# Gates and their output products as [token, column], and a 512-wide hi/lo product in the feed-forward inputs of a four-layer network on one core

## The chip, the cores and the metric

One NeuronCore of a Trainium2 chip runs the whole program. The metric is the device time of one execution in microseconds (us).

## The reference, cut to what matters

Two blocks of two layers each work on 256 tokens of 1024 columns, in float32. Every layer ends in the same two stages: gated attention branches that are mixed and projected back into the residual stream, and a feed-forward network.

```
# block 1 (layers 0, 1)
proj = rms_norm(x) @ w_in                       # 7984 columns for the attentions, then m_a, m_b (1024 each)
y_ret = (silu(g_r) * o_r) @ w_o_ret             # 2048 -> 1024
y_nsa = o_n @ w_o_nsa                           # 1024 -> 1024
x = x + (sigmoid(m_a)*y_ret + sigmoid(m_b)*y_nsa) @ w_out
a, b = split(rms_norm(x) @ w_ffn_in)            # 2 x 2816 columns
x = x + (silu(a) * b) @ w_ffn_out
# block 2 (layers 0, 1)
gates = sigmoid(gl)                             # three gates of 1024 columns
merged = sum over a, b, c of gate * (y @ w_br)  # each y: 512 -> 1024
x = x + merged @ w_out
x = x + square(relu(rmsnorm(x) @ w_up)) @ w_down        # 4096 columns
x = x + sigmoid(rmsnorm(x) @ w_ple_gate) * (p @ w_ple_proj)
```

## The kernel before, in words

**Three products for one.** Every float32 operand is split into `hi`, its value rounded to float32r, and `lo`, the rest. A product is then hi·hi + hi·lo + lo·hi, three float32r products added up in a PSUM bank. A weight piece of 512 KB is loaded by SP's DMA queue (`load`, L365), rounded into `whi` by ScalarE (ACT) and subtracted into `wlo` by VectorE (DVE) (`split_weight`, L377; the operations themselves stand at L169 and L183). `execute` (L391) writes out the program item by item; it splits pieces up to `LOOK` = 2 items ahead of their use. There are 5 raw and 6 split buffers.

**Two layouts.** `proj_T` (L442) keeps the weight stationary and streams the activations: per 128 rows and 128 columns of weight three products of 256 tokens each, and two column tiles share one bank of [128, 2, 256]. Its output is [column, token]. A unit of 256 columns on 1024 rows takes 8 x 2 x 3 = 48 products. `proj_N` (L479) keeps the activations stationary and streams 512 weight columns: the output is [token, column], one bank for each of the two token tiles t; 512 columns on 1024 rows take 8 x 2 x 3 = 48 products. `Down` (L526) has the form of `proj_N` with four banks [t][column half] that live through the whole feed-forward stage; `bulk` adds pieces as the hidden chunks come, `ends` does the last eight row tiles, first for column half 0, then for half 1. In the profile "b<-u,whi" is a product with stationary `whi` and streamed `u` (`proj_T`), "b<-whi,u" one with stationary `u` and streamed `whi` (`proj_N`, `Down`). PSUM has eight banks (`bank`).

**Block 1's gates** (`block1_layer`, L743; the stage begins after the heads). `ev_ma`, `ev_mb` put tanh(m/2) aside, `ev_yr` and `ev_yn` multiply (1 + tanh) with the branch's bank; the second adds the first, halves the sum and splits it into `mixT`, an `Act` of [column, token] that `w_out` then takes as its stationary operand. All four projections are `proj_T`; w_o_ret has 16 row tiles, the others 8. **Block 2's gates** (`block2_layer`, L1268: `ev_gates`, `ev_br`, `gates`, `branch`) do the same with three gates (8 row tiles) and three branches (4 row tiles).

**Feed-forward inputs.** Block 1: columns 0 to 255 of a and b go together through `proj_N`, which covers the transposes of the norm; the other ten chunks of 256 columns are `proj_T` units, a (evicted by Silu on ACT) and then b (multiplied from the bank on DVE, then split). Block 2: columns 0 to 511 by `proj_N`, then fourteen `proj_T` units (Relu on ACT, square on DVE, split).

**Norms and turns.** `Norm` (L594) scales x to [token, column]; `turn` transposes 128 x 128 blocks on TensorE (PE, L250) and splits them from PSUM into the hi and lo tiles of the next stream (hT, hF, hP), which are `u` tiles: the pool has 17 of 4 KB a partition. `first_turn` stands ahead of the last weight piece of the product before it; it also sets `order_after`, behind which later weight splits are issued.

**Order.** The instructions of each engine run in the order in which the program issues them. `Beside` (L291) holds generators for the small work (attention heads, transposes of results). `pump` advances them after every item by the planner's own costs; `until` and `finish` advance them until something is done. `begin` (L678) starts the kernel: x's first token tile on SP's queue, the norm's row and x's second token tile on ACT's queue, a constant, three warm-up products and two products that spread the norm's row over the partitions.

Of the kernel before, what the change touches and what calls it, by code (L numbers as in the profile page):

```python
# [18 lines left out]
D = 1024  # L19
# [62 lines left out]
NB_RAW, NB_HI, NB_U, NB_Z, NB_W, NB_S = 5, 6, 17, 6, 8, 24  # L82
# [20 lines left out]
def tile_kernel(ctx: ExitStack, tc: tile.TileContext, A: dict, out: bass.AP):  # L103
# [11 lines left out]
    def u(shape, dt=F32):  # L115
        return up.tile(shape, dt, name="u", tag="u", bufs=NB_U)

# [321 lines left out]

    S = {}  # L440

# [37 lines left out]
    def proj_N(w2d, c0, c, x, nkt, evac, runs=1, stride=0, tmajor=False, between=None, turn=None):  # L479
# [9 lines left out]
        def fn(pc, j, k0, nk, tt_):  # L489
            if tmajor and j == len(ks) - 1 and tt_ == (0,) and between is not None:  # L490
                between()
            for t in tt_:
# [33 lines left out]
    class Down:  # L526
# [26 lines left out]
        def ends(self, f, norm, turn=None):  # L553
# [4 lines left out]
            for j in pairs:  # L558
                def fn(pc, j=j):
                    for kk in range(2):  # L560
# [81 lines left out]

    def new_norm(row, key):

        def f():
            S["norm"] = Norm(row, None if key is None else Act(8))
            if key is not None:
                S["next", key] = S["norm"].dst
        do(f)
# [27 lines left out]

    def begin():  # L678
# [10 lines left out]
        consts(cp, 0)  # L689
# [4 lines left out]
        S["norm"] = Norm(None, Act(8), g=g)  # L694
# [48 lines left out]
    def block1_layer(i):  # L743
# [372 lines left out]
        def part(o, c):  # L1116
            if c % 2 == 0:
                o[c // 2] = u([128, 4, 256])
            return o[c // 2][:, 2 * (c % 2):2 * (c % 2) + 2, :]

        def half_of(o, c):
            return o[c // 2][:, 2 * (c % 2):2 * (c % 2) + 2, :]

        def ev_ma(c):
            def f(ci, acc):
                ma[c] = w2([128, 2, 256])
                act(ma[c], acc, AF.Tanh, scale=0.5)
            return f

        def ev_yr(c):  # L1130
            def f(ci, acc):
                stt(out=part(M, c), in0=ma.pop(c), scalar=1.0, in1=acc, op0=OP.add, op1=OP.mult)
            return f

        def ev_mb(ci, acc):
            act(part(G, ci), acc, AF.Tanh, scale=0.5)

        def ev_yn(c, acc):
            s = w2([128, 2, 256])
            stt(out=s, in0=half_of(G, c), scalar=1.0, in1=acc, op0=OP.add, op1=OP.mult)  # L1140
            tt(out=s, in0=s, in1=half_of(M, c), op=OP.add)
            cs = slice(2 * (c % 2), 2 * (c % 2) + 2)
            m = S["mixT"]
            split(s, m.hi[c // 2][:, cs, :], m.lo[c // 2][:, cs, :], 0.5)
# [17 lines left out]
        dn.ends("mixT", norm, lambda: first_turn("hF"))  # L1162
# [40 lines left out]
        def ev_a(ci, acc):  # L1203
            R["s"] = w2([128, 2, 256])
            act(R["s"], acc, AF.Silu)

        def ev_b(c):
            def f(ci, acc):
                s = R["s"]
                tt(out=s, in0=s, in1=acc, op=OP.mult)  # L1210
# [57 lines left out]
    def block2_layer(i):  # L1268
# [353 lines left out]
        def part(o, c):  # L1622
            if c % 2 == 0:
                o[c // 2] = u([128, 4, 256])
            return o[c // 2][:, 2 * (c % 2):2 * (c % 2) + 2, :]

        def half_of(o, c):
            return o[c // 2][:, 2 * (c % 2):2 * (c % 2) + 2, :]

        def ev_gates(b, raw):  # L1630
            def f(c, acc):
                if raw:
                    copy_a(part(G[b], c), acc)
                else:
                    act(part(G[b], c), acc, AF.Tanh, scale=0.5)
            return f

        def tanh_gates():
            for j in range(2):
                act(G["b"][j], G["b"][j], AF.Tanh, scale=0.5)  # L1640

        def ev_br(b):
            def f(c, acc):
                m = part(M, c) if b == "b" else w2([128, 2, 256])
                stt(out=m, in0=half_of(G[b], c), scalar=1.0, in1=acc, op0=OP.add, op1=OP.mult)
# [208 lines left out]
```

## Time and profile before

| | us |
|---|---|
| runs of the kernel before | 2163.63 median of 3 (2163.18 to 2164.15) |
| the profiled execution's own time | 2162.97 |
| its span in the profile | 2161.0 |
| PE busy | 2135.8 |
| DVE busy | 1488.0 |
| ACT busy | 1235.0 |

The granted clock of the span is 1.00 of 2.4 GHz. A product's duration in the profile (284 ns for one of 256 columns) holds the time through the array; products overlap, so what one costs is the distance from its start to the next one's. In the timeline, neighbouring instructions of one form are merged ("x2"), and the start is that of the first.

### The profile page before, as it was taken

To read this page: it belongs to the slowest core of one execution; us is meant where nothing else is said; L and a number is where in the kernel's file an instruction comes from. 1 tells how busy PE (TensorE), PEld (TensorE's weight loads), DVE (VectorE), ACT (ScalarE), POOL (GpSimd) and SP (SyncE) were. 2 spreads that over 40 slices of the span, in tenths; PEclk is the share of its full clock that TensorE was granted. 3 is DMA by queue.
4 is the path that set the end of the run, shared out by engine and by line. 5 is a ranking of instruction groups with operands and counts; after the bars stand their busy time and mean duration, and the time that the engine had idled before them with its cause. 6 is when DMAs were issued, how large, how long until landed. Compare 5 with 4: busy or idle time off the path is not lost.

```text
span 2161.0 us, 37493 instructions
## 1 busy us (share of the span) xinstructions
PE 2135.8 (99%) x14688; PEld 1952.0 (90%) x14688; DVE 1488.0 (69%) x2774; ACT 1235.0 (57%) x2044; POOL 97.8 (5%) x115
## 2 busy tenths in 40 slices
PE   9999999999999999999999999999999999999998
PEld 7898899899988889998997999998997999998997
DVE  6687865655577787666556897876557887876555
ACT  5476754544456666545445777755445777655443
POOL 1000000000000000000000010100000010100000
PEclk9999999999999999999999999999999999999999
DMA  9655555566585554555555645556655545455653
GB/s 284 204 157 145 150 166 168 185 187 188 175 261 156 150 156 136 167 192 176 185 186 167 185 126 161 159 173 197 186 186 172 171 136 176 152 185 179 191 186 108
DMA packets 298271, 376.49 MB, mean 174 GB/s; under 512 B 16364, under 2 KB 238588, under 8 KB 298094
## 3 DMA queue, kind: packets, MB, share of 16 engines
q1 hardware_dynamic: 296140, 369.07, 55.3%
q0 software_dynamic: 1664, 4.50, 1.2%
q8 instruction: 115, 1.88, 0.4%
q10 hardware_dynamic: 290, 0.53, 0.1%
q14 instruction: 62, 0.51, 0.1%
HBM read 372.93 MB, written 1.11 MB: 173 GB/s over the span
## 4 chain that ended last, share of the span: by engine, by line
PE 83%; DVE 10%; ACT 3%; issue 2%; POOL 1%; DMA 0%; POOLq 0%; SPq 0%; DVEq 0%; ACTq 0%
PE b L216 80%; DVE wlo L183 3%; PE b L250 3%; DVE u L183 2%; DVE w L183 1%; POOL s L239 1%; ACT z L169 1%; ACT u L169 1%; ACT whi L169 1%; DVE z L194 1%; DVE w L194 0%; DVE s L208 0%; DVE z L183 0%; ACT L169 0%; DVE z L1408 0%
## 5 line engine op out<-in xcount | busy, mean ns | idle before, releaser
L183 DVE TENSOR_TENSOR wlo<-raw,whi 128x1024 fp32r<-128x1024 f32 (+1 forms) x670 | 815.1, 1221 | 428.2 <-ACT whi L169 421.6
L169 ACT ACTIVATE whi<-raw 128x1024 fp32r<-128x1024 f32 (+1 forms) x670 | 704.9, 1056 | 655.2 <-PE b L216 460.6
L216 PE MATMUL b<-u,whi 128*128 128x256 f32 x5760 | 1049.3, 284 | 0.0
L216 PEld LDWEIGHTS b<-u,whi 128*128 128x128 f32 x5760 | 900.4, 192 | 9.5 <-issue 4.9
L216 PE MATMUL b<-u,wlo 128*128 128x256 f32 x2880 | 814.7, 283 | 0.0
L216 PE MATMUL b<-whi,u 128*128 128x512 f32 (+2 forms) x2752 | 809.1, 371 | 0.2
L216 PEld LDWEIGHTS b<-whi,u 128*128 128x128 f32 x2752 | 500.8, 189 | 88.6 <-issue 4.9
L216 PEld LDWEIGHTS b<-u,wlo 128*128 128x128 f32 x2880 | 552.0, 192 | 0.0
L216 PE MATMUL b<-wlo,u 128*128 128x512 f32 (+2 forms) x1376 | 508.4, 369 | 0.0
L216 PEld LDWEIGHTS b<-wlo,u 128*128 128x128 f32 x1376 | 259.9, 189 | 39.0 <-DVE wlo L183 0.9
L169 ACT ACTIVATE u<-b 64x512 fp32r<-64x512 f32 (+3 forms) x234 | 134.0, 579 | 86.7 <-PE b L250 44.4
L169 ACT ACTIVATE z<-z,s 128x256 f32<-128x256 f32 (+2 forms) x304 | 123.6, 425 | 25.5 <-DVE s L203 22.6
L239 POOL TENSOR_TENSOR s<-s,mhalf 128x1 f32<-128x1 f32 (+3 forms) x60 | 70.5, 1174 | 1491.8 <-DVE s L194 1060.2
L183 DVE TENSOR_TENSOR u<-b,u 128x512 fp32r<-128x512 f32 (+2 forms) x150 | 98.3, 665 | 12.0 <-ACT u L169 9.3
L169 ACT ACTIVATE w<-b 128x512 f32<-128x512 f32 (+3 forms) x150 | 81.1, 546 | 44.4 <-PE b L216 43.9
L250 PE MATMUL b<-const,w 128*128 128x128 f32 (+1 forms) x416 | 64.2, 279 | 11.3 <-DVE w L194 10.3
L250 PEld LDWEIGHTS b<-const,w 128*128 128x128 f32 (+1 forms) x416 | 47.7, 141 | 24.2 <-issue 13.7
L169 ACT ACTIVATE u<-w 128x512 fp32r<-128x512 f32 x80 | 49.5, 620 | 10.1 <-DVE w L183 9.9
L183 DVE TENSOR_TENSOR w<-w 128x512 f32<-128x512 f32 (+3 forms) x94 | 51.9, 566 | 3.3 <-ACT w L169 3.2
L169 ACT ACTIVATE w<-x 128x512 f32<-128x512 f32 x44 | 27.4, 623 | 32.6 <-DVE x L183 30.6
L216 PE MATMUL b<-u 128*128 128x256 f32 (+1 forms) x288 | 40.8, 287 | 3.4 <-DVE u L183 3.4
L183 DVE TENSOR_TENSOR u<-w,u 128x512 fp32r<-128x512 f32 x64 | 43.8, 685 | 0.0
(147 smaller groups left out, 1198.4 us busy)
## 6 DMA issues: line engine op xcount, KB each, us to landing
raw<-w_in SPq DMA_DIRECT2D x268, 512.0 KB, 3.8
raw<-w_ffn_in SPq DMA_DIRECT2D x80, 512.0 KB, 3.5
raw<-w_up SPq DMA_DIRECT2D x64, 512.0 KB, 3.7
raw<-w_down SPq DMA_DIRECT2D x64, 512.0 KB, 3.5
raw<-w_ffn_out SPq DMA_DIRECT2D x44, 512.0 KB, 3.6
raw<-w_o_ret SPq DMA_DIRECT2D x32, 512.0 KB, 3.5
raw<-w_out SPq DMA_DIRECT2D x32, 512.0 KB, 3.6
raw<-w_o_nsa SPq DMA_DIRECT2D x16, 512.0 KB, 3.4
```

Source lines behind the costliest of these rows:

```text
L169: nc.scalar.activation(o, i, func, bias=bias, scale=scale, accum_out=accum_out)
L183: nc.vector.tensor_tensor(out=out, in0=in0, in1=in1, op=op)
L194: nc.vector.scalar_tensor_tensor(out=out, in0=in0, scalar=scalar, in1=in1, op0=op0, op1=op1)
L216: nc.tensor.matmul(o, lhsT, rhs, start=start, stop=stop, skip_group_check=True)
L239: nc.gpsimd.tensor_tensor(o, i, mhalf[:, :n], op=OP.pow)
L250: nc.tensor.transpose(o, i, C("ident")[:i.shape[0], :i.shape[0]])
```

## The change: what it does

- `proj_T2` with `Stream` and `both_halves`: in the feed-forward inputs of both blocks, `whi` meets hi and lo of the stream in one 512-wide product, and `wlo` meets hi in a 256-wide one into the first half of the bank. There is a bank for each of the two column tiles, so two for a unit. The eviction copies the second half (ACT) and adds it to the first (DVE), for each bank. Block 2's Relu and square become one DVE operation.
- `Stream` lays hi and lo of the normed stream side by side in two tiles of a pool of their own (`xt`, two buffers of 8 KB a partition); the `u` pool shrinks from 17 to 13 buffers.
- Gates and branch products of both blocks become `proj_N` with 512 columns. `Mix` transposes the gated sums (four 128 x 128 transposes for each token tile and column half) and splits them into `mixT`; `need` makes `w_out`'s first pass wait for its half.
- `begin`: x's second token tile goes to SP's queue behind the first two weight pieces; the first norm's scaling is put ahead of the first weight split on DVE (`order_after`), and the second token tile's norm behind the first turn's last ACT instruction.

```diff
-NB_RAW, NB_HI, NB_U, NB_Z, NB_W, NB_S = 5, 6, 17, 6, 8, 24
+NB_RAW, NB_HI, NB_U, NB_X, NB_Z, NB_W, NB_S = 5, 6, 13, 2, 6, 8, 24
...
+    class Stream:
+        def __init__(self):
+            self.b = [xt([128, 2, 4, 256]) for _ in range(2)]
+            self.hi, self.lo = ([z[:, j] for z in self.b] for j in range(2))
...
+        def HL(self, k):
+            return self.b[k // 4][:, :, k % 4, :]
...
+    def proj_T2(w2d, c0, x, evac):
+        box = {}
+        for k0 in range(0, 8, 4):
+            def fn(pc, k0=k0):
+                if k0 == 0:
+                    box["b"] = [bank([128, 2, 256]) for _ in range(2)]
+                hi, lo = pc
+                for k in range(4):
+                    kk = k0 + k
+                    for ct in range(2):
+                        cs = slice(128 * ct, 128 * ct + 128)
+                        o = box["b"][ct]
+                        mm(o, hi[:, k, cs], S[x].HL(kk), kk == 0, False)
+                        mm(o[:, 0, :], lo[:, k, cs], S[x].H(kk), False, kk == 7)
+                if k0:
+                    evac(box["b"])
+            items.append(Item(fn, spec(w2d, 128 * k0, 4, c0, 256)))
+
+    def both_halves(banks):
+        s, h = w2([128, 2, 256]), w2([128, 2, 256])
+        for ct, b in enumerate(banks):
+            copy_a(h[:, ct, :], b[:, 1, :])
+            tt(out=s[:, ct, :], in0=b[:, 0, :], in1=h[:, ct, :], op=OP.add)
+        return s
...
+    class Mix:
+        def __init__(self):
+            S["mixT"], self.done = Act(8), set()
+        def turn(self, t, c, s):
+            def g():
+                yield
+                b = bank([128, 4, 128])
+                for q in range(4):
+                    transpose(b[:, q, :], s[:, 128 * q:128 * q + 128])
+                ts_ = slice(128 * t, 128 * t + 128)
+                split(b, S["mixT"].hi[c][:, :, ts_], S["mixT"].lo[c][:, :, ts_], 0.5)
+                self.done.add((t, c))
+                yield
+            bg.add(g(), True)
+        def need(self, k):
+            bg.until(lambda: all((t, k // 4) in self.done for t in range(2)))
...
     def begin():
-        for q, t in ((nc.sync, 0), (nc.scalar, 1)):
-            if t:
-                row = u([1, D])
-                q.dma_start(row, A["norm_mix_g"][0:1, :])
-            for c in range(2):
-                q.dma_start(x[:, t, 512 * c:512 * c + 512], xin[:, t, 512 * c:512 * c + 512])
+        row = u([1, D])
+        nc.scalar.dma_start(row, A["norm_mix_g"][0:1, :])
+        load_x(0)
+        consts(cp, 0)
+        for it in [z for z in items if z.spec is not None and not z.spec[-1]][:2]:
+            with tc.issue_after(last_of(mybir.EngineType.SP)):
+                it.pc = load(it.spec)
+        with tc.issue_after(last_of(mybir.EngineType.SP)):
+            load_x(1)
...
-        for c in range(4):
-            proj_T(w, 7984 + 256 * c, 256, "hT", 8, ev_ma(c))
-            if c:
-                proj_T(A["w_o_ret"][i], 256 * (c - 1), 256, "ret", 16, ev_yr(c - 1), pre=need_ret if c == 1 else None)
-        proj_T(w, 9008, 256, "hT", 8, ev_mb)
-        proj_T(A["w_o_ret"][i], 768, 256, "ret", 16, ev_yr(3))
-        for c in range(1, 4):
-            proj_T(w, 9008 + 256 * c, 256, "hT", 8, lambda ci, acc, c=c: ev_mb(c, acc))
+        for c in range(2):
+            proj_N(w, 7984 + 512 * c, 512, "hT", 8, ev_ma(c))
+            proj_N(A["w_o_ret"][i], 512 * c, 512, "ret", 16, ev_yr(c), pre=None if c else need_ret)
+        for c in range(2):
+            proj_N(w, 9008 + 512 * c, 512, "hT", 8, ev_mb(c))
         do(bg.finish)
-        do(lambda: S.update(mixT=Act(8)))
-        proj_T(A["w_o_nsa"][i], 0, 1024, "onT", 8, ev_yn)
+        do(lambda: S.update(mix=Mix()))
+        for c in range(2):
+            proj_N(A["w_o_nsa"][i], 512 * c, 512, "onT", 8, ev_yn(c))
...
-        dn.ends("mixT", norm, lambda: first_turn("hF"))
+        dn.ends("mixT", norm, lambda: first_turn("hF"), lambda j: S["mix"].need(j))
...
-                proj_T(wi, 256 * c, 256, "hF", 8, ev_a)
-                proj_T(wi, FFN + 256 * c, 256, "hF", 8, ev_b(c))
+                proj_T2(wi, 256 * c, "hF", ev_a)
+                proj_T2(wi, FFN + 256 * c, "hF", ev_b(c))
...
-                r = w2([128, 2, 256])
-                act(r, acc, AF.Relu)
-                tt(out=r, in0=r, in1=r, op=OP.mult)
+                r = both_halves(banks)
+                stt(out=r, in0=r, scalar=0.0, in1=r, op0=OP.max, op1=OP.mult)
...
+    def first_norm():
+        norm().both(0)
+        order_after[:] = [last_of(mybir.EngineType.DVE), last_of(mybir.EngineType.Activation)]
+
+    def second_norm():
+        with tc.issue_after(last_of(mybir.EngineType.Activation)):
+            norm().both(1)
```

## Rows read from the trace of the kernel before

**Rows 1.** The page: busy time of the engines, and the chain that ended last by engine.

```profile
PE 2135.8 (99%) x14688; PEld 1952.0 (90%) x14688; DVE 1488.0 (69%) x2774; ACT 1235.0 (57%) x2044; POOL 97.8 (5%) x115
...
PE 83%; DVE 10%; ACT 3%; issue 2%; POOL 1%; DMA 0%; POOLq 0%; SPq 0%; DVEq 0%; ACTq 0%
```

**Rows 2.** Waits of PE: waiting, releaser, us in total, times, longest.

```profile
PE b L250 <- DVE w L194: 10.3, 12, 3.4
```

**Rows 3.** Groups by form: line, engine, out<-in, stationary, streamed, count | busy us, mean ns.

```profile
L216 PE MATMUL b<-u,whi 128*128 128x256 f32 x5760 | 1049.3, 284 | 0.0
...
L216 PE MATMUL b<-u,wlo 128*128 128x256 f32 x2880 | 814.7, 283 | 0.0
...
L216 PE MATMUL b<-whi,u 128*128 128x512 f32 x2176 | 698.7, 393 | 0.2
...
L216 PE MATMUL b<-wlo,u 128*128 128x512 f32 x1088 | 426.1, 392 | 0.0
```

**Rows 4.** Timeline, PE, block 1's second layer, in a `proj_T` stretch.

```profile
900.00 0.40 PE L216 MATMUL b<-u,whi 128*128 128x256 f32 x2
...
904.68 0.40 PE L216 MATMUL b<-u,whi 128*128 128x256 f32 x2
```

**Rows 5.** Timeline, PE, in a `Down` stretch of the feed-forward stage.

```profile
429.71 0.62 PE L216 MATMUL b<-whi,u 128*128 128x512 f32 x2
...
432.43 0.62 PE L216 MATMUL b<-whi,u 128*128 128x512 f32 x2
```

**Rows 6.** Timeline, PE, a `proj_N` stretch in block 1's attention stage.

```profile
61.73 0.40 PE L216 MATMUL b<-whi,u 128*128 128x512 f32 x1
...
64.25 0.39 PE L216 MATMUL b<-whi,u 128*128 128x512 f32 x1
```

**Rows 7.** Timeline, PE, block 2: products whose streamed operand lies in two parts.

```profile
1234.98 1.11 PE L216 MATMUL b<-u,later 128*128 128x512 f32 x6
1235.93 0.40 PE L216 MATMUL b<-u,whi 128*128 128x256 f32 x2
```

**Rows 8.** Windows of the feed-forward stages: length, then busy us (instructions) by engine.

```profile
420.00:590.00 170.00, 170.00 (x1189) 159.81 (x1189) 87.70 (x86) 73.93 (x86) 0.55 (x1) 1.00 0.60 189
...
1480.00:1638.00 158.00, 158.00 (x994) 143.49 (x994) 86.60 (x88) 73.36 (x88) 0.55 (x1) 1.00 0.58 187
```

**Rows 9.** Groups by form: a copy and an addition out of PSUM, and the weight's subtraction.

```profile
L183 DVE TENSOR_TENSOR wlo<-raw,whi 128x1024 fp32r<-128x1024 f32 x664 | 809.0, 1222 | 428.2 <-ACT whi L169 421.6 <-PE b L250 4.0
...
L183 DVE TENSOR_TENSOR w<-b,const 128x256 f32<-128x256 f32 x8 | 3.4, 422 | 4.2 <-PE b L216 4.2
...
L169 ACT ACTIVATE w<-b 128x256 f32<-128x256 f32 x8 | 3.0, 379 | 0.6 <-PE b L216 0.5
```

**Rows 10.** Timeline, PE, block 2, as its first `w_out` begins: four transposes between products.

```profile
1417.34 0.60 PE L250 MATMUL b<-const,w 128*128 128x128 f32 x4
...
1417.69 0.48 PE L216 MATMUL b<-whi,u 128*128 128x512 f32 x1
1418.00 0.39 PE L216 MATMUL b<-wlo,u 128*128 128x512 f32 x1
```

**Rows 11.** Timeline: `w_out` of the first layer begins on PE; the last gate chain ends on DVE.

```profile
380.81 0.40 PE L216 MATMUL b<-whi,u 128*128 128x512 f32 x1
...
383.48 0.68 DVE L194 SCALAR_TENSOR_TENSOR u<-w,u 128x512 fp32r<-128x512 f32 x1
```

**Rows 12.** Timeline of the kernel's first 14 us, all engines.

```profile
2.10 6.09 SPq L372 DMA_DIRECT2D raw<-w_in  x8
...
4.46 3.78 PE L216 MATMUL b<-u,ones 1*128 1x512 f32 x4
...
9.73 1.23 DVE L183 TENSOR_TENSOR wlo<-raw,whi 128x1024 fp32r<-128x1024 f32 x1 [4.08 <-ACT whi L169]
...
10.87 1.40 DVE L194 SCALAR_TENSOR_TENSOR w<-x,s,b 128x512 f32<-128x512 f32 x2
...
13.47 0.79 PE L216 MATMUL b<-whi,u 128*128 128x512 f32 x1
```

More of the change, by code (lines that the diff above doesn't have):

```diff
@@ L477, in part_N, with proj_N @@
         mm(acc, xx.L(kk)[:, s], hi[:, k, :], False, kk == nkt - 1)
-    def proj_N(w2d, c0, c, x, nkt, evac, runs=1, stride=0, tmajor=False, between=None, turn=None):
+    def proj_N(w2d, c0, c, x, nkt, evac, runs=1, stride=0, tmajor=False, between=None, turn=None, pre=None):
         n = c * runs
@@ L491, in fn @@
                 between()
+            if pre is not None:
+                pre(k0)
             for t in tt_:
@@ L551, in bulk, with ends @@
                 items.append(Item(fn, spec(self.w, 128 * k, 1, 0, 1024)))
-        def ends(self, f, norm, turn=None):
+        def ends(self, f, norm, turn=None, pre=None):
             k0 = self.n - self.tail
@@ L559, in fn @@
                 def fn(pc, j=j):
+                    if pre is not None:
+                        pre(j)
                     for kk in range(2):
@@ L641, in add @@
                     self.then.both(t)
+    class Mix:
[14 more added lines that the diff above has]
+            bg.until(lambda: all((t, k // 4) in self.done for t in range(2)))
     def new_norm(row, key):
         def f():
-            S["norm"] = Norm(row, None if key is None else Act(8))
-            if key is not None:
-                S["next", key] = S["norm"].dst
+            S["norm"] = Norm(row, Stream())
+            S["next", key] = S["norm"].dst
         do(f)
@@ L693, in begin @@
             mm(g[c], ones, row[:, 512 * c:512 * c + 512], True, True)
-        S["norm"] = Norm(None, Act(8), g=g)
+        S["norm"] = Norm(None, Stream(), g=g)
         S["next", "hT"] = S["norm"].dst
@@ new lines, in ev_yr, with ev_mb, f, ev_yn @@
+            return f
+        def ev_mb(c):
+            def f(t, acc):
+                if t == 0:
+                    G[c] = u([128, 2, 512])
+                act(G[c][:, t, :], acc, AF.Tanh, scale=0.5)
+            return f
+        def ev_yn(c):
+            def f(t, acc):
+                s = w2([128, 512])
+                stt(out=s, in0=G[c][:, t, :], scalar=1.0, in1=acc, op0=OP.add, op1=OP.mult)
+                tt(out=s, in0=s, in1=M[c][:, t, :], op=OP.add)
+                S["mix"].turn(t, c, s)
+            return f
@@ L1634, in f @@
                 else:
-                    act(part(G[b], c), acc, AF.Tanh, scale=0.5)
+                    act(G[b][c][:, t, :], acc, AF.Tanh, scale=0.5)
             return f
         def tanh_gates():
[L1639 to L1645, printed above, removed]
+            for c in range(2):
+                act(G["b"][c], G["b"][c], AF.Tanh, scale=0.5)
@@ L1646, in f, with ev_br @@
+        def ev_br(b, c):
+            def f(t, acc):
+                if b == "b":
+                    if t == 0:
+                        M[c] = u([128, 2, 512])
+                    m = M[c][:, t, :]
+                else:
+                    m = w2([128, 512])
+                stt(out=m, in0=G[b][c][:, t, :], scalar=1.0, in1=acc, op0=OP.add, op1=OP.mult)
                 if b == "c":
-                    tt(out=half_of(M, c), in0=half_of(M, c), in1=m, op=OP.add)
+                    tt(out=M[c][:, t, :], in0=M[c][:, t, :], in1=m, op=OP.add)
@@ L1648, in f @@
                 if b == "a":
-                    tt(out=m, in0=half_of(M, c), in1=m, op=OP.add)
-                    if c == 0:
-                        S["mixT"] = Act(8)
-                    cs = slice(2 * (c % 2), 2 * (c % 2) + 2)
-                    mt = S["mixT"]
-                    split(m, mt.hi[c // 2][:, cs, :], mt.lo[c // 2][:, cs, :], 0.5)
+                    tt(out=m, in0=M[c][:, t, :], in1=m, op=OP.add)
+                    if t == 0 and c == 0:
+                        S["mix"] = Mix()
@@ L1655, in ev_br, with branch @@
+                    S["mix"].turn(t, c, m)
             return f
         def gates(b, raw=False):
-            proj_T(w, 4932 + 1024 * "abc".index(b), 1024, "hT", 8, ev_gates(b, raw))
-        def branch(b, c0=0, n=4):
-            e = ev_br(b)
-            proj_T(A[f"w_br_{b}_2"][i], 256 * c0, 256 * n, "y" + b, 4, lambda ci, acc: e(c0 + ci, acc))
+            for c in range(2):
+                proj_N(w, 4932 + 1024 * "abc".index(b) + 512 * c, 512, "hT", 8, ev_gates(b, c, raw))
+        def branch(b):
+            for c in range(2):
+                proj_N(A[f"w_br_{b}_2"][i], 512 * c, 512, "y" + b, 4, ev_br(b, c))
@@ L1705, in block2_layer @@
         dn.bulk(range(8 - TAIL), "mixT")
-        dn.ends("mixT", norm, lambda: first_turn("hF"))
+        dn.ends("mixT", norm, lambda: first_turn("hF"), lambda j: S["mix"].need(j))
         nch = DFF // 256
@@ L1813, in tile_kernel @@
     open_pool("block1")
[L1814 removed]
+    def first_norm():
[4 more added lines that the diff above has]
+            norm().both(1)
+    do(first_norm)
     lead = len(items)
     first_turn("hT")
[L1817 removed]
+    do(second_norm)
     do(block1_constants)
```

67 lines of the change are left out of this document (28 added, 39 removed).

## The prediction, written before the changed kernel was run

> **What bounds the kernel now.** I begin with the page's busy times [rows 1]: PE is busy for 2135.8 of 2161.0 us, DVE for 1488.0, ACT for 1235.0. Busy alone would not do, since the ends of products are modelled, so the waits of PE come next. The longest entry is 10.3 us over twelve waits for the scaled stream at the turns of the norms [rows 2]; nothing else is of that size. The chain that ended last runs through PE for 83% [rows 1]. So PE's own pace sets the time nearly everywhere, and a change is worth what it takes off or puts on PE, unless another engine falls behind.
>
> That pace is not in the durations of the groups (284 ns, 393 ns [rows 3]), because products overlap. It is in the distance of starts. From 900.00 to 904.68 us lie 13 triples, 39 products of 256 columns: 4.68 / 39 = 120.0 ns each [rows 4]. From 429.71 to 432.43 us lie 4 triples, 12 products of 512 columns: 226.7 ns each [rows 5]. Two narrow products thus take 240.0 and one wide one 226.7: at the 2.4 GHz that is granted (1.00 in both windows of rows 8) 256 columns are 106.7 ns of streaming, and some 13 ns come with each product, whatever its width.
>
> **Counting the products.** Rows 3 give 5760 + 2880 = 8640 products in the form of `proj_T`, 180 units of 48.
> - Feed-forward inputs: block 1 has 10 chunks x 2 (a, b) x 2 layers = 40 units, block 2 has 14 x 2 = 28. In each of these 68 units 16 triples of 256 become a 512 and a 256. That is one product fewer for each triple, 68 x 16 = 1088.
> - Gates and branches: in block 1 a layer has 4 units for m_a, 8 for w_o_ret (16 row tiles), 4 for m_b, 4 for w_o_nsa; in block 2 12 for the gates and 6 for the branches (4 row tiles). Both layers: 40 + 36 = 76 units, in which 48 products of 256 become 24 of 512: 76 x 24 = 1824 fewer.
>
> Together 2912 merges, with the streamed columns unchanged. At 13.3 ns this would be 38.7 us. In a stage with more traffic the wide products are slower: 61.73 to 64.25 us holds 11 in 2.52 us, 229 ns [rows 6]. The stages that change are nearer to the quiet one in kind (a few large operations on DVE and ACT), so I take 228: 12 ns x 2912 = **-34.9 us**. The wide product of the feed-forward streams an operand in two parts 4 KB apart. The nearest form is the product with `later`, two of 512 and four of 256 in 0.95 us [rows 7]; with the narrow ones at 120 the wide ones are at 235 each. Its price is therefore 227 to 235, and I keep 228, as the small group follows other work of that stage; 235 stays for the range.
>
> **Transposes of Mix.** Two token tiles x two halves x four layers = 16 groups of four. Such a group takes 0.35 us to the next product, and the product behind it 0.31 us where 0.23 is usual [rows 10]: 0.35 + 0.08, so **+7.0 us** for 16 (5.7 if two groups stand together and the pace returns at once). The splits behind them take the place of splits of the same size before.
>
> **The wait of Mix.** `w_out`'s fifth row tile needs half 1. Before, the last gate chain ended at 384.2 us for products that had begun at 380.81 [rows 11], and row tiles 6 and 7 came three pieces later, 3 x 12 x 227 ns = 8.2 us. Now half 1 is wanted after two pieces, 5.4 us, plus the 0.7 us of the transposes, and the chain is longer: two DVE operations of 0.69 for each token tile, the transposes (which the planner puts behind the first piece, 2.7 us), then two copies on ACT and two subtractions on DVE with a weight piece among them. That ends at about 5 to 6 us. Behind a late ACT copy stand the weight copies of the next pieces, and PE waits for these after its two pieces of lead. I take 0.25 us for each of the four layers, **+1.0**; ends 0 and +4.
>
> **Eviction of the feed-forward units.** Two copies of 0.38 us on ACT and two additions of 0.42 on DVE, the second waiting for the first [rows 9]: for a unit +0.84 us on DVE, +0.76 on ACT (in block 2 the Relu goes instead). PE needs none of it soon: the hidden chunk is used a unit or more later. On DVE weight subtractions of 1.22 us queue behind an addition that waits, and PE takes these pieces. The cover is large: in 420 to 590 us DVE is busy for 87.7 of 170 us and ACT for 73.9 [rows 8]; 20 units add 16.8 and 15.2. **0**, as long as two pairs of banks are free, see the rivals.
>
> **Stream and the pools.** The two `xt` tiles are the 16 KB that four of the seventeen `u` held, so the other work keeps its 13. hF is written long after hT's last use. In one place, block 2 from its first layer to the second, hT is written while the last piece with hP still runs, six products or 1.4 us [rows 5]; if the buffer is only handed over then, the turn comes later by up to 2 us. **+0.7**; ends 0 and +2.
>
> **The start.** DVE subtracts the first weight at 9.73 and scales x only at 10.87, and the first product of the layer starts at 13.47 [rows 12]. The spread of the norm's row ends on PE at 8.24 [rows 12], so with the scaling put first it could run its halves from about 6.5 and 8.3. Both halves and the first weight would be done by 8.3 + 0.7 + 1.23 = 10.2 in place of 10.87 + 1.40 = 12.3: some 2 us ahead. The moved transfers: eight weight issues take 6.09 us on SP's queue [rows 12], 0.76 each; the first two pieces (two issues each) come 3.0 us ahead of x's second tile, which is wanted only by the second turn. POOL's queue moves past nothing. **-2.0**; ends -4 (the weight's landing no longer last either) and +1 (the second tile late).
>
> **Sum**: -34.9 + 7.0 + 1.0 + 0.7 - 2.0 = -28.2. Against the profiled execution's 2162.97 us: 2134.8. The median of the runs stands 0.66 above that execution, which makes **2135.4 us**.
>
> **Ends.** Best: 38.7 off, transposes 5.7, no stall, start -4: 2162.97 - 37.0 + 0.66 = 2126.6. Worst: 5 ns on 1088 and 11 ns on 1824 merges, 25.5 off, then +7.0 +4 +2 +1: 2152.1. So 2126 to 2152.
>
> **Rivals.**
> - *The merged product streams as two* (chance 0.06). Two separated parts would cost 240 as before, and the feed-forward gains nothing: 1088 x 12 ns = 13.1 us come back, 2148.5. Rows 7 speak against it, at 235 or less; they are few.
> - *Merging hardly pays* (0.04). The other terms sum to +6.7 us; if a merge saved 2.3 ns, they would eat it, and the time would stay at 2163.6. It takes a wide product of 238 ns where rows 5 have 226.7 and the slowest group 235. The Trainium skill, "TensorE: Matmul & The Clock Gate", section "Back-to-back issue gap", has this rule: at the full clock a gap is the columns at 2.4 GHz plus 2.5 ns. By it a merge gives 2.5 ns, 7.3 us in all, and the kernel would stay where it is (an estimate from that page). The trace does not agree: the addition is 13 ns, not 2.5, at both widths.
> - *The feed-forward runs out of banks* (0.05), the case on the slower side. `Down` holds four of the eight, a unit now needs two. Place: the first product of each of the 68 units. If only one pair came free, it would wait for the unit before: a copy and two additions, 0.38 + 0.42 + 0.42 = 1.2 us behind the last product [rows 9], without a weight piece between. 68 x 1.2 = 82 us, so 2217. It decides from 28.2 / 68 = 0.41 us a unit. Against it: four are left, two pairs, and between two uses of a pair lies a unit of 16 x (228 + 120) ns = 5.6 us, against an eviction of 1.2 us and at most two weight pieces of 1.22.
> - *Queues eat a third* (0.10): the chains of Mix and the turns hit at their upper ends, and the start brings nothing. With +4, +2 and +1 the sum is -20.9, 2142.7.
>
> **How the numbers follow.** My forecast has 0.75, the four rivals 0.25. The range of 2126 to 2152 takes in the first and the last rival. About 0.2% (4.3 us) is what a measurement here can tell from no change. Faster: forecast, first and last rival, 0.91. Same: the second, 0.04. Slower: the third, 0.05.
>
> **What would show it.** The page should have 14688 - 2912 + 64 = 11840 products, with 1088 wide ones from `xt` and as many narrow ones. Their starts should lie 348 ns apart for a pair: 360 would be the first rival. `proj_T` should be left with 36 units, 1728 products. PE's waits should stay near 10 us at the turns. A wait of PE for DVE's additions out of the banks, with holes at the starts of units, would be the third rival, and one for Mix's subtractions in `w_out` the fourth. The first product of the layer should start at about 11 us. A wide product above 235 ns, or DVE busy for over 80% of a feed-forward stage, would make the prediction wrong.

## The result, and the profile after

The changed kernel takes **2141.32 us** (median of 4 runs, 2140.73 to 2143.80), the kernel before 2163.68 beside it on the same chip: a ratio of 0.9901, 95% interval 0.9889 to 0.9913, 22.4 us less. Forecast were 2135.4, in 2126 to 2152. The profiled execution is the slowest of the four, 2143.80 us with a span of 2141.8; against the profiled execution of before the spans differ by 19.2 us, and this is what the traces must account for.

The page of the changed kernel, busy times and the chain that ended last by engine, to be held against [rows 1]:

```profile
PE 2117.3 (99%) x11840; PEld 1801.8 (84%) x11840; DVE 1537.7 (72%) x2910; ACT 1258.0 (59%) x2152; POOL 97.9 (5%) x115
...
PE 83%; DVE 10%; ACT 2%; issue 2%; DMA 1%; POOL 1%; SPq 0%; POOLq 0%; DVEq 0%; ACTq 0%
```

The products are the 11840 that were counted. DVE is busy for 50 us more, and PE is still the engine that is busy for 99% of the span. The waits of PE, as in [rows 2]:

```profile
PE b L253 <- DVE w L197: 7.4, 11, 2.1
PE b L219 <- DVE u L186: 3.9, 4, 1.4
PE b L219 <- ACT w L172: 1.6, 3, 0.7
...
PE b L219 <- DVE wlo L186: 1.5, 2, 0.9
PE b L219 <- ACT xt L172: 0.9, 1, 0.9
```

The turns still lead with 7.4 us in 11 (10.3 in 12 before). A wait for an addition out of the feed-forward banks would be one of L219 for DVE w. There is one of that name, of 0.4 us at 1221.16, in block 2's gates of b among the heads' products; in the four feed-forwards PE waits for no addition. The groups by form, as in [rows 3]:

```profile
L219 PE MATMUL b<-xt,wlo 128*128 128x256 f32 x1664 | 468.4, 281 | 0.0
L219 PE MATMUL b<-xt,whi 128*128 128x512 f32 x1088 | 386.1, 398 | 0.0
...
L219 PE MATMUL b<-xt,whi 128*128 128x256 f32 x1152 | 211.0, 285 | 0.0
```

1088 wide products, 1088 narrow ones beside them, and 36 units of `proj_T` (1152 + 576 products). What a pair costs stands in the timeline, PE in the first feed-forward stage:

```profile
428.66 0.40 PE L219 MATMUL b<-xt,whi 128*128 128x512 f32 x1
428.90 0.28 PE L219 MATMUL b<-xt,wlo 128*128 128x256 f32 x1
429.02 0.40 PE L219 MATMUL b<-xt,whi 128*128 128x512 f32 x1
...
431.84 0.40 PE L219 MATMUL b<-xt,whi 128*128 128x512 f32 x1
```

Nine pairs from 428.66 to 431.84: **353.3 ns** a pair, where 348 were forecast and 227 + 120 = 347 is the sum of the two paces of before [rows 4, 5]. From the start of a wide product to that of the narrow one go 236.5 ns on average in this stage, and 116.7 from there to the next wide one. The windows of a feed-forward stage of each block, units and second product, in block 2 with the `proj_N` stretch ahead of them (length; busy us of PE, PEld, DVE, ACT, POOL; granted clock, DMA share, GB/s), as in [rows 8]:

```profile
409.95:584.24 174.29, 174.29 (x915) 148.65 (x914) 107.86 (x131) 89.16 (x131) 0.55 (x1) 1.00 0.64 199
1442.63:1623.34 180.71, 180.30 (x905) 152.06 (x904) 117.36 (x141) 89.53 (x125) 1.96 (x2) 1.00 0.63 192
```

DVE is busy for 62% of the first. To see where the time went, I cut both traces at the products at which the same number of weight columns has been streamed, and take the length of each stage. "Predicted" is the forecast's own terms for that stage (12 ns a merge, 0.43 us a group of four transposes, 0.25 us for a wait of Mix):

| stage | before, us | after, us | predicted | measured |
|---|---|---|---|---|
| block 1, layer 0: end of the first stage | 29.94 | 27.49 | -2.0 | -2.45 |
| rest of that layer's attention | 214.49 | 214.48 | 0 | -0.01 |
| block 1: m_a, w_o_ret, m_b, two layers | 113.34, 113.33 | 109.13, 109.06 | -9.2 | -8.5 |
| block 1: w_o_nsa, two layers | 23.04, 23.04 | 22.65, 22.65 | -0.6 | -0.8 |
| block 2: gates and branches, two layers | 129.86, 129.95 | 126.43, 127.48 | -8.6 | -5.9 |
| w_out, four layers | 22.70, 22.70, 22.68, 22.68 | 23.55 each | +4.4 | +3.4 |
| feed-forward from the first unit on, block 1 | 176.30, 177.96 | 174.29, 175.83 | -7.7 | -4.1 |
| block 2's feed-forward, with its `proj_N` stretch | 182.25, 182.23 | 180.71, 180.67 | -5.4 | -3.1 |
| block 2: the first two stages of each layer | 47.96, 46.53 | 49.90, 46.83 | +0.7 | +2.2 |

The stages left out differ by 0.05 us at most. The measured column sums to -19.2, all of it. The largest miss is the feed-forward: -7.2 for -13.1.

### The profile page after: what moved, and what is told of

Its sections match the earlier page's. It is cut to its first block, busy times and chain, and to the rows that moved or that the text cites. A ratio compares the mean times of both kernels' runs of the same rounds, so it can differ in the third digit from the quotient of the medians.

```text
span 2141.8 us, 32029 instructions
## 1 busy us (share of the span) xinstructions
PE 2117.3 (99%) x11840; PEld 1801.8 (84%) x11840; DVE 1537.7 (72%) x2910; ACT 1258.0 (59%) x2152; POOL 97.9 (5%) x115
## 3 DMA queue, kind: packets, MB, share of 16 engines
q8 instruction: 93, 1.52, 0.3%
## 4 chain that ended last, share of the span: by engine, by line
PE 83%; DVE 10%; ACT 2%; issue 2%; DMA 1%; POOL 1%; SPq 0%; POOLq 0%; DVEq 0%; ACTq 0%
PE b L219 80%; DVE wlo L186 3%; PE b L253 3%; DVE w L186 2%; DVE u L186 1%; POOL s L242 1%; DMA w<-idx_k_norm 1%; ACT z L172 1%; ACT w L172 1%; DMA raw<-w_in 0%; ACT whi L172 0%; ACT u L172 0%; DVE xt L186 0%; DVE w L197 0%; DVE s L211 0%
## 5 line engine op out<-in xcount | busy, mean ns | idle before, releaser
L219 PE MATMUL b<-whi,xt 128*128 128x512 f32 (+2 forms) x2240 | 656.6, 369 | 1.1 <-ACT xt L172 0.9
L219 PE MATMUL b<-xt,whi 128*128 128x256 f32 (+1 forms) x2240 | 597.1, 340 | 0.0
L219 PE MATMUL b<-whi,u 128*128 128x512 f32 x1728 | 551.4, 392 | 0.0
L219 PE MATMUL b<-xt,wlo 128*128 128x256 f32 x1664 | 468.4, 281 | 0.0
L219 PEld LDWEIGHTS b<-whi,xt 128*128 128x128 f32 x2240 | 405.8, 190 | 71.9 <-issue 6.6
L219 PEld LDWEIGHTS b<-xt,whi 128*128 128x128 f32 x2240 | 384.0, 190 | 53.9 <-issue 2.1
L219 PE MATMUL b<-wlo,xt 128*128 128x512 f32 (+2 forms) x1120 | 410.2, 366 | 1.5 <-DVE wlo L186 1.5
L219 PEld LDWEIGHTS b<-whi,u 128*128 128x128 f32 x1728 | 324.5, 188 | 68.2 <-issue 0.3
L219 PE MATMUL b<-wlo,u 128*128 128x512 f32 x864 | 336.9, 390 | 0.0
L219 PEld LDWEIGHTS b<-xt,wlo 128*128 128x128 f32 x1664 | 315.8, 190 | 1.6
L219 PEld LDWEIGHTS b<-wlo,xt 128*128 128x128 f32 x1120 | 212.5, 190 | 32.7 <-DVE wlo L186 3.7
L219 PEld LDWEIGHTS b<-wlo,u 128*128 128x128 f32 x864 | 162.4, 188 | 30.9
```

The source lines that it names most:

```text
L219: nc.tensor.matmul(o, lhsT, rhs, start=start, stop=stop, skip_group_check=True)
```

## The experiments

"The changed kernel" is 2141.32 us throughout. All ratios are to the kernel before, with 95% intervals.

### The three parts, each by itself

The kernel before with the gates, `Mix` and `need` alone; with `Stream` and `proj_T2` alone; with the new start alone. Relative to the changed kernel, the first two take back:

```diff
-                proj_T2(wi, 256 * c, "hF", ev_a)
+                proj_T(wi, 256 * c, 256, "hF", 8, ev_a)
```

```diff
-        for c in range(2):
-            proj_N(A["w_o_nsa"][i], 512 * c, 512, "onT", 8, ev_yn(c))
+        proj_T(A["w_o_nsa"][i], 0, 1024, "onT", 8, ev_yn)
...
-        dn.ends("mixT", norm, lambda: first_turn("hF"), lambda j: S["mix"].need(j))
+        dn.ends("mixT", norm, lambda: first_turn("hF"))
```

> The kernel before with the gates' part alone (proj_N, Mix, need); feed-forward, stream tiles and start as before. By the forecast's terms: -21.9 (1824 merges x 12 ns) + 7.0 + 1.0 = -13.9 us, about 2149.8. By the stages of the changed kernel's trace (gates, branches and w_out together -11.7): about 2152. If the gates are what fell short, -8 or less.

> The kernel before with the feed-forward part alone (Stream, proj_T2, both_halves, pools). By the forecast: -13.1 + 0.7 = -12.4 us, about 2151.3. Theory that the merged pair costs 353 ns and not 348: 1088 x (360 - 353) = -7.6, about 2156. Rival that banks run out or that the evictions are not hidden: at or above 2163.

> The kernel before with the start alone (order of x, first weights, first norm). By the forecast -2.0 us, 2161.7; by the trace (first product 4.4 us earlier, the end of the first values stage 2.7 us earlier) -2.7. Rival: the earlier products run at the lower clock level and the second token tile lands late, so nothing is left: 2163.7 within 1.

Gates alone: 2152.65 us, ratio 0.9949 (0.9936 to 0.9961), 11.0 us. Feed-forward alone: 2156.71, 0.9969 (0.9957 to 0.9981), 6.9 us. Start alone: 2163.25, 0.9998 (0.9989 to 1.0007), 0.4 us. The three sum to 18.3 us where the whole change gave 22.4; each has an interval of 2 to 3 us to either side, so this does not show that the parts help each other. The first two repeat the stages of the table: -4.23, -0.39 and +0.85 us in m_a to m_b, w_o_nsa and w_out of the first layer; -2.11, -2.01, -1.54, -1.52 in the four feed-forwards. The start alone ends the first stage at 26.80 us in its profile, 3.1 before that of the kernel before (the other two profiles with the old start have 28.89 and 29.04), and 2.1 us are left at the gates of that layer. Then they are lost: it has 27.11 and 28.28 us for the stage of bq and bk in block 2 where before had 25.70 and 26.47. The waits of PE in that profile:

```profile
PE b L216 <- DVE u L183: 7.2, 7, 2.6
PE b L250 <- DVE w L194: 6.9, 11, 2.1
```

DVE u has 7.2 us here, 3.4 in the kernel before and 3.9 in the changed kernel. In the other thirteen profiles of this study the stage of bq and bk lies between 25.3 and 26.8 us. So the early start is worth some 2 us where it is made; why that stage was so long in this one kernel I did not find.

### Where the streamed operand lies

The two parts of the streamed operand beside each other, so that the 512 columns are contiguous:

```diff
-            self.b = [xt([128, 2, 4, 256]) for _ in range(2)]
-            self.hi, self.lo = ([z[:, j] for z in self.b] for j in range(2))
+            self.b = [xt([128, 4, 2, 256]) for _ in range(2)]
+            self.hi, self.lo = ([z[:, :, j, :] for z in self.b] for j in range(2))
...
-            return self.b[k // 4][:, :, k % 4, :]
+            return self.b[k // 4][:, k % 4, :, :]
```

> The changed kernel with hi and lo of a row tile next to each other ([4, 2, 256] in place of [2, 4, 256]), so that the wide product streams 512 columns in a row. Theory A, the two parts 4 KB apart cost the pair its 6 ns: pairs at 347 ns, 1088 x 6 = -6.5 us against the changed kernel, about 2135. Theory B, it is the alternation of a wide and a narrow product, or C, the traffic of DVE and ACT: pairs stay at 353, 2141.

2141.62 us, 0.9897 (0.9883 to 0.9910). PE's timeline, nine pairs in 3.18 us as before:

```profile
428.93 0.40 PE L219 MATMUL b<-xt,whi 128*128 128x512 f32 x1
...
432.11 0.40 PE L219 MATMUL b<-xt,whi 128*128 128x512 f32 x1
```

The split operand costs nothing here. The 235 ns of [rows 7] were not its price, and they are the slow case: the trace of before has eight such groups, and six of them go like this one, 0.93 us for two wide and four narrow products, with the wide ones 231 to 232 ns apart.

```profile
1266.57 1.09 PE L216 MATMUL b<-u,later 128*128 128x512 f32 x6
1267.50 0.28 PE L216 MATMUL b<-whi,u 128*128 128x256 f32 x1
```

### The order of wide and narrow

Per weight piece, first all eight wide products, then all eight narrow ones:

```diff
-                for k in range(4):
-                    kk = k0 + k
-                    for ct in range(2):
+                for narrow in range(2):
+                    for k in range(4):
+                        kk = k0 + k
+                        for ct in range(2):
...
```

> The changed kernel with the products of a weight piece in another order: its eight wide ones, then its eight narrow ones. Theory B (each change from a wide to a narrow product and back costs about 6 ns): 2 changes in place of 16 a piece, pairs on average near 347 ns, 1088 x 6 = -6.5 us against the changed kernel, 2135. Theory C (traffic of the other engines): 353 as before, 2141.

2137.86 us, 0.9881 (0.9865 to 0.9898). PE's timeline of the same stretch:

```profile
428.73 2.00 PE L219 MATMUL b<-xt,whi 128*128 128x512 f32 x8
430.57 1.12 PE L219 MATMUL b<-xt,wlo 128*128 128x256 f32 x8
431.52 1.78 PE L219 MATMUL b<-xt,whi 128*128 128x512 f32 x7
```

Eight wide ones take 1.84 us, 230 each, and eight narrow ones 0.95, 119 each. The four feed-forwards are 172.70, 174.33, 179.57 and 179.57 us, 5.3 less together. So the order carried the price. Next, single alternation again, but with the narrow product always in the other bank than the wide one ahead of it:

```diff
...
+                wide(0, 0)
+                for k in range(4):
+                    wide(k, 1)
+                    narrow(k, 0)
+                    if k < 3:
+                        wide(k + 1, 0)
+                    narrow(k, 1)
```

> The changed kernel with wide and narrow products still alternating, but each product goes to the other bank than the one before it. Theory D (a narrow product that adds to the bank the wide one has just written is held up): pairs at 347 ns, -6.5 us, 2135. Theory B (the change of width itself): 353, 2141.

2140.50 us, 0.9896 (0.9882 to 0.9911). The pairs stay at 352 ns and the feed-forwards are only 0.4 to 0.5 us shorter each. So the price is not that of a narrow product held up by the wide one ahead of it in the same bank. Its expectation went too far, though, in saying that each product goes to the other bank than the one before it: here the wide product behind a narrow one goes to the bank of that narrow one, so a bank is still written twice in a row once a pair, at the other of the two steps. The times did not move with it: 235 ns from a wide start to a narrow one and 117 from there to the next wide one, where the changed kernel has 236.5 and 116.7. And `proj_T` writes one bank 48 times in a row at 120.0 ns a product [rows 4]. This speaks against the bank, but an alternation that never writes a bank twice in a row was not run. Last, two wide products, then two narrow ones:

```diff
-                    for ct in range(2):
-                        cs = slice(128 * ct, 128 * ct + 128)
-                        o = box["b"][ct]
-                        mm(o, hi[:, k, cs], S[x].HL(kk), kk == 0, False)
-                        mm(o[:, 0, :], lo[:, k, cs], S[x].H(kk), False, kk == 7)
+                    for narrow in range(2):
+                        for ct in range(2):
+                            cs = slice(128 * ct, 128 * ct + 128)
+                            o = box["b"][ct]
+                            if narrow:
+                                mm(o[:, 0, :], lo[:, k, cs], S[x].H(kk), False, kk == 7)
+                            else:
+                                mm(o, hi[:, k, cs], S[x].HL(kk), kk == 0, False)
```

> As the changed kernel, but the products of a unit in the order wide, wide, narrow, narrow (both banks, then both banks), so half the changes of width are left (544 wide-to-narrow in place of 1088; the run with 8 and 8 has 136). Theory B (each change of width costs the same, 5.3 us / 952 = 5.6 ns): -3.0 us in the four feed-forwards together, 0.9, 0.8, 0.65 and 0.65 us each, 2138 to 2139 us, and a pair costs some 350 ns. Rival (the cost goes with narrow products standing singly or in short runs, not with the number of changes): no gain, stages 174.3, 175.8, 180.8, 180.8 us as in the changed kernel. Rival 2 (a single narrow product behind a wide one is what costs, so that two and two already escape it): all of it, -5.3 us, as with 8 and 8.

**2136.90 us**, 0.9876 (0.9861 to 0.9891). PE's timeline, and the window of the first feed-forward:

```profile
428.70 0.63 PE L219 MATMUL b<-xt,whi 128*128 128x512 f32 x2
429.16 0.40 PE L219 MATMUL b<-xt,wlo 128*128 128x256 f32 x2
429.39 0.63 PE L219 MATMUL b<-xt,whi 128*128 128x512 f32 x2
...
431.48 0.62 PE L219 MATMUL b<-xt,whi 128*128 128x512 f32 x2
```

```profile
409.11:581.55 172.44, 172.44 (x916) 147.89 (x914) 106.02 (x131) 89.01 (x131) 0.55 (x1) 1.00 0.63 201
```

Eight pairs from 428.70 to 431.48: 347.5 ns a pair, the 347 of the separate paces. The feed-forwards are 172.44, 174.11, 179.38 and 179.41 us, 6.2 less than in the changed kernel and 13.4 less than before. The medians of the runs lie 4.4 us apart, within their intervals of some 3 us each. With half the changes of width left all of the price is gone; with an eighth of them left, in 8 and 8, no more than that was. So my theory of a price for each change of width falls, and the second rival of its expectation stands: what costs, 353.3 - 347.5 = 5.8 ns a pair, is that wide and narrow products stand *singly*. Whether the single narrow one or the single wide one is to blame was not separated, and what in PE makes it so, no row shows.

### Evictions and banks

Every eviction of a unit done twice (two copies and two additions for each bank, the same results):

```diff
-            copy_a(h[:, ct, :], b[:, 1, :])
-            tt(out=s[:, ct, :], in0=b[:, 0, :], in1=h[:, ct, :], op=OP.add)
+            for _ in range(2):
+                copy_a(h[:, ct, :], b[:, 1, :])
+                tt(out=s[:, ct, :], in0=b[:, 0, :], in1=h[:, ct, :], op=OP.add)
```

> The changed kernel with each copy and each addition of the evictions done twice (the second gives the same values): +0.84 us on DVE and +0.76 us on ACT for each of 68 units, 57 us of DVE in all. If the evictions are hidden behind PE: 2141 within 2. If DVE or ACT sets the pace of the feed-forward stages: up to +57.

2142.37 us, 0.9902 (0.9887 to 0.9917); the first two feed-forwards last 174.31 and 175.83 us as in the changed kernel, the others 0.2 more. The window of the first:

```profile
409.95:584.24 174.29, 174.29 (x914) 148.64 (x913) 121.00 (x173) 101.19 (x171) 0.55 (x1) 1.00 0.63 199
```

DVE has 13 us more in it, ACT 12, PE not one hole. The eviction is hidden with room to spare. Then one pair of banks taken away for the feed-forward:

```diff
+            if c == 2:
+                hold_banks("held", True)
...
+        hold_banks("held", False)
```

> The changed kernel with two of the eight banks held through the feed-forward loops, so that a unit has one pair of banks: the third rival of the prediction made real. Where a unit follows a unit directly (in block 1 b after a, and a after b once the bulk pieces have run out, 11 a layer; in block 2 the last unit alone; 24 in all) it waits for a copy and two additions, 1.2 us and the hand-overs: 24 x 1.2 to 1.6 = +29 to +38 us, about 2170 to 2180. If two pairs were short already, little changes: 2141 to 2145.

2141.90 us, 0.9903 (0.9889 to 0.9918), but it tested nothing. DVE's timeline of that run:

```profile
423.38 0.07 DVE L487 MEMSET b<- 128x8 f32 x1
424.04 0.20 DVE L201 COPY s<-b 128x8 f32<-128x8 f32 x1
```

The copy that was to release the bank after the last chunk ran 0.7 us behind the hold, since nothing made it wait. The second attempt makes the release read the last hidden chunk:

```diff
-                    copy_v(small([128, 8]), b[:, :8])
+                    tt(out=small([128, 8]), in0=b[:, :8], in1=S["hid"].f[max(S["hid"].f)][:, 1, 1, :8].bitcast(F32), op=OP.add)
```

> As the changed kernel, but from the third group of columns of each feed-forward on two PSUM banks are held, and their release now needs the last hidden part of that feed-forward (in the run before this one the release could be issued right behind the hold, at 424.1 us of the trace, so nothing was held and 2141.90 us came out). One pair of banks is left for the units. Theory (the prediction's bank rival is a real price that this kernel escapes by its second pair): a unit that follows a unit directly, about 9 in each layer of block 1 and none in block 2, where a stretch of the second product lies between, waits for the copy and the sum of both banks, 1.0 to 1.6 us each: 18 x 1.0 to 1.6 = +18 to +29 us, so 2159 to 2171 us, with PE waiting for DVE w at the products' line some 18 times; the block 2 feed-forwards unchanged at 180.9 us. Rival (the rival as the prediction priced it): 68 units wait 1.2 us each, +82 us, 2223 us. Rival 2 (the evictions are quick enough even so): below +5 us.

2151.08 us, 0.9940 (0.9923 to 0.9957), 9.8 more than the changed kernel; the feed-forwards of block 1 are 4.2 and 4.6 us longer, those of block 2 by 0.2. The place was right (block 1, a unit behind a unit), the price half of what I gave or less: 4.2 us over 9 units are 0.5 each, where I had 1.0 to 1.6. PE's timeline between two units, and its waits in the whole kernel:

```profile
448.42 0.28 PE L219 MATMUL b<-xt,wlo 128*128 128x256 f32 x1
448.53 0.40 PE L219 MATMUL b<-whi,u 128*128 128x512 f32 x1
448.76 0.40 PE L219 MATMUL b<-wlo,u 128*128 128x512 f32 x1
449.00 0.39 PE L219 MATMUL b<-whi,u 128*128 128x512 f32 x1
449.28 0.50 PE L219 MATMUL b<-xt,whi 128*128 128x512 f32 x1
...
540.81 0.50 PE L219 MATMUL b<-xt,whi 128*128 128x512 f32 x1 [0.80 <-DVE w L186]
```

```profile
PE b L219 <- DVE w L186: 4.3, 7, 0.8
```

In most chunks three products of the second feed-forward product now stand between the two units and fill the 0.75 us; such a chunk is 0.2 us longer than in the changed kernel (16.97 for 16.79). Most of the 4.2 us, 3.3, falls on the end of the loop, where in the changed kernel six units follow each other without a break: at three of them PE waits, by 0.6 to 0.8 us, 2.0 together. The waits of 4.3 us in the whole kernel are less than half of the 9.8, and where the rest lies I did not find. So the bank rival is real, but it needs one pair, and then costs 10 us and not 82.

### Merging the other 36 units

The units of queries, keys and compressed keys merged too, first all 36 (with the order 8 and 8), then only the eight of bq and bk in block 2 (with two and two):

```diff
...
-                        evac(ci, box["b"])
+                        evac(ci, both_halves(box["b"]))
```

> As the grouped order (8 wide products, then 8 narrow ones, 2137.86 us), and the 36 further units that lie as [column, token] on the normalized stream (queries, keys, rotated pairs, compressed keys) merged in the same way: one wide and one narrow product in place of three narrow ones, in two banks, both halves copied and added before the old eviction. Theory (the product count decides): 16 x 36 = 576 times 3 x 120.0 against 229.8 + 119.0 ns = -11.2 ns each, -6.5 us, less small waits: 2130 to 2134 us; stages with two such units shorter by 0.36 us each. Rival (eviction and banks take it back): 72 copies of 0.37 us on ACT and 72 sums of 0.42 us on DVE come into stages where DVE is busy 64 to 97 % and the units' readers wait some 0.8 us longer, and a third bank per unit is missing to the heads beside: 2137 to 2150 us, with new PE waits for DVE in the query and key stages of block 2 (28 of 28 us busy on DVE there).

> As the order wide, wide, narrow, narrow (2136.90 us), and of the 36 further units on the normalized stream only the eight of block 2 (bq and bk, four in each layer) are merged in the same way; the 28 of block 1, whose layers lost 2.4 us together when all 36 were merged (+3.3 and -0.9 us), stay as they are. Theory (only the product count and the end of the single alternation count): 128 times 3 x 120.0 against 347 ns = -13 ns each, -1.7 us: 2135.2 us, taken up in the stage of the bq and bk products, which is 0.4 us shorter in each layer beyond what its waits vary, and nothing elsewhere. Rival (block 2 gains by the shift of the heads beside, as it seemed to when all 36 were merged: its layers were 2.4 and 1.8 us shorter): -4.2 us, 2132.7 us, most of it outside that stage, in the stages of branch b and the gates. Rival 2 (the 16 copies and sums come into stages where DVE is the busier one and give it back): 2136.5 to 2138 us.

All 36: 2136.65 us, 0.9874 (0.9859 to 0.9889), not to be told from 2137.86 without them and between what the two sides expected. Against that kernel block 1's attention is 1.8 and 5.5 us shorter, but the gates behind it are 3.0 longer in each layer and w_o_nsa 1.4: work of the heads that lay in the attention before is now issued there (48 transposes of the heads in the first layer's gates for 42). Only eight: 2138.97 us, 0.9891 (0.9875 to 0.9908), where 2136.90 stood without them; the intervals overlap, but there is surely no gain of 4 us. The stage of bq and bk is 0.5 and 0.2 us shorter, where 64 merges of 13 ns would be 0.8 in each layer (the expectation put 0.4 on it). The gates of b in the second layer are 3.7 longer, those of c in the first 2.0, and other stages of block 2 moved by 1 to 3 us either way. PE's timeline in the gates of b:

```profile
1699.99 0.49 PE L219 MATMUL b<-u,later 128*128 128x512 f32 x1
1701.60 1.20 PE L219 MATMUL b<-u,later 128*128 128x512 f32 x6 [1.11 <-DVE u L186]
1703.61 0.62 PE L219 MATMUL b<-u,later 128*128 128x512 f32 x2 [0.80 <-DVE u L186]
```

PE waits for two subtractions of the heads beside, 1.9 of the 3.7 us. None of the three expectations of the last run held; the third came nearest. Merging a unit whose readers wait is not worth its count. Of what was run, the order two and two is the simplest of the fastest.

## Why the prediction was right, and where it was off

- **What bounds the kernel.** Right: PE's own pace. 2912 merges with all that hangs on them took 11.7 + 7.2 us off, and doubling the evictions on the other engines changed nothing.
- **The merges of the feed-forward inputs**, -13.1 in the sum: this is the step that failed. It added the pace of a wide product to the pace of a narrow one, both read in stretches of one width, and put 348 on a pair. Alternating, a pair takes 353.3, and the stages gave 7.2 us. In the order two and two the same products take 347.5 and give 13.4. The number was right for an order that the change does not have. The bound of 235 that the prediction kept from [rows 7] covered the miss (5 ns a merge at the low end), for a reason that the contiguous operand refutes. The prediction also named a wide product above 235 ns as a sign of being wrong. By its starts it takes 236.5, with 116.7 for the narrow one, so the sign came up, and it points at this term.
- **The merges of the gates and branches**, -21.9, +7.0 and +1.0, -13.9 together: measured -11.7. In block 1's stage with 384 merges a merge gave 4.2 / 384 = 11.0 ns, for 12. Block 2 gave 5.9 for 8.6. There the heads run beside; in the gates of a in the first layer the stage fell by 0.4 us for 1.15, and PE's waits in it are

```profile
PE b L219 <- DVE u L186: 1.4, 1, 1.4
PE b L219 <- ACT w L172: 0.7, 1, 0.7
```

  2.1 us, where the kernel before had 1.3 and 0.2. Part of what PE saved there may now be waiting for the heads; this was not tested by itself.
- **Transposes of Mix**, +7.0: right. w_out, with two groups in it, is 0.84 to 0.87 us longer in all four layers, 0.42 to 0.43 a group, as [rows 10] had it.
- **Wait of Mix**, +1.0: it does not exist; the 0.84 to 0.87 leave no room for it, and PE waits for nothing in any of the four w_out stages.
- **Eviction**, 0: right, shown by doubling it.
- **Stream and the pools**, +0.7: +2.2 in this execution, of which +0.5 comes back in every kernel. In the second layer of block 2 the first stage takes 20.54 to 20.58 us in all eleven kernels with `Stream`, the feed-forward part alone among them, and 20.02 to 20.06 in the three without. In the first layer that stage takes 22.2 without, but 22.2 to 23.8 among kernels with it; what decides there I did not find.
- **The start**, -2.0: right where it is made. The first product began earlier than forecast, at 9.04 for 11. In part that is this execution: the two products that spread the norm's row took 2.16 us, not the 3.78 of [rows 12]. With 3.78 the run with two and two starts at 9.97 and ends the first stage at 26.62, against 29.94 before. The start of the profiled execution:

```profile
4.46 2.16 PE L219 MATMUL b<-u,ones 1*128 1x512 f32 x4
...
5.93 1.48 DVE L197 SCALAR_TENSOR_TENSOR w<-x,s,b 128x512 f32<-128x512 f32 x2 [0.66 <-POOL s L242]
...
9.04 0.79 PE L219 MATMUL b<-whi,xt 128*128 128x512 f32 x1 [0.92 <-ACT xt L172]
```

  Of 4.4 us at the first product 2.45 were left at the end of the first stage. By its own runs the start alone gave 0.4 us, which is no difference clear of noise: what it gains in the first stage was not shown at the end of the kernel.
- **Rivals.** The product that streams as two would have 360 a pair; 353.3 rules it out. "Merging hardly pays" had 2.3 ns a merge; 360 - 353.3 = 6.7 in this order and 12.5 in the best one rule it out. By the rule of the Trainium skill for a product by itself ("TensorE: Matmul & The Clock Gate", "Back-to-back issue gap") a pair would take 325 ns, 320 of columns and 5 of gaps (an estimate from that page). The trace does not agree: the best order measured has 347.5. The bank rival was built and costs 10 us. The queues' rival, at 2142.7, came nearest to the time but by other terms: Mix does not wait, and the start does gain in its own stage.

## What to carry to other kernels

A pace read in a run of equal products holds for runs of equal products. Where a merge leaves wide and narrow ones, put at least two of a width behind each other, and read the pair's pace before you count. Count merges only where nothing else waits on the unit: 36 more of them, with heads beside, gave nothing.

## What the runs showed of the hardware that was not expected

A product of 512 columns and one of 256 that alternate singly take 353.3 ns a pair; two and two take 347.5, eight and eight 349 (230 + 119). The pairs are not even: starts of wide products lie some 0.35, 0.35 and 0.36 us apart in turn.

The granted clock was not 1.00 at the beginning of every execution. The windows of the changed kernel from 4 to 16 us (columns as above):

```profile
4.00:8.00 4.00, 3.81 (x14) 1.68 (x12) 1.64 (x3) 1.63 (x5) 0.55 (x1) 1.00 0.97 292
8.00:12.00 4.00, 3.08 (x8) 1.87 (x7) 3.46 (x4) 2.53 (x4) 0.00 (x0) 0.53 1.05 366
12.00:16.00 4.00, 4.00 (x13) 3.06 (x12) 1.71 (x4) 3.23 (x6) 0.55 (x1) 0.61 1.05 310
```

For most of 8 to 16 us the lower of the two levels, 1.2 GHz, is granted. It goes with what PE did just before: in the five profiles of fourteen in which the two products that spread the norm's row took 2.09 to 2.37 us, the clock of 8 to 12 us is 0.52 to 0.59; in the nine in which they took 3.77 or 3.78 it is 1.00. Which of the two comes first, and why an execution takes the one or the other way, stays open, and so does the price: from the first product of the layer to the first one of its first unit go 18.23 us here and 16.42 with two and two, but also 18.20 in the run with all 36 units merged, at 1.00.
